# A decoder layer with product-key experts: one weight tile instead of two in the expert loop, seven gathered-row buffers instead of five, and another eviction order

## The chip, the cores and the metric

The kernel runs on one core of a Trainium2 chip. The metric is the device time of one execution in microseconds. Before the change it is 2859.01 us, the median of three runs (2856.11 to 2863.37).

## What is computed

One layer of a decoder on 1024 tokens of width 1024: RMS norm, four retention heads and four differential attention heads, an output projection with a residual, then a product-key expert layer (PEER) and a final norm. The change touches the expert layer alone:

```
def peer(xn, wq, subkeys, u, v):
    ...
        q = (xb @ wq).reshape(t, PEER_HEADS, 2, PEER_DQ // 2)
        s = jnp.einsum('thpd,hpkd->thpk', q, subkeys).astype(jnp.float32)
        s_top, i_top = lax.top_k(s, K)
        ...
        e = i1 * N_KEYS + i2
        g = jax.nn.softmax(c_top, axis=-1)
        ue = jnp.take(u, e, axis=0)
        ve = jnp.take(v, e, axis=0)
        act = jax.nn.gelu(jnp.einsum('thkd,td->thk', ue, xb).astype(jnp.float32), approximate=False)
        return jnp.einsum('thk,thkd->td', (g * act).astype(xb.dtype), ve)
```

Each token picks 8 x 16 = 128 of 16384 single-neuron experts; `u` and `v` have a row of 1024 floats for each.

## The kernel before

The eight tiles of 128 tokens go two ways. Three tiles are **sparse** (`ST`): POOL gathers for each of the 128 picks one row of `u` per token (line 869, a 128x1024 tile), and VectorE multiplies it with the token and sums (line 871); after a Gelu the rows of `v` follow (line 876), and VectorE adds each, times its weight, to the accumulator `sa` (line 878). All gathered rows live in the pool tag `ug` with five buffers; a gather waits until the update that reads the buffer's last row is done. Five tiles are **dense** (`DT`, 640 tokens): all 16384 experts are computed for them, in 128 blocks of 128 experts (a block is called an expert in the code), and a weight matrix G, zero where an expert was not picked, masks the result.

Two stages matter here. In the **G stage** (about 1010 to 1290 us) `dense_routes` and `build_g` make G: for eight tokens at a time VectorE makes one-hot tiles `oh` (lines 586 to 593, ScalarE helps on line 590), TensorE multiplies them (line 601) into a PSUM bank `psG` with four tokens of 128x128 each, and ScalarE evicts the bank into `st` (line 603), whose layout is expert block, then 32 tokens. `st` goes to DRAM as `g_d` (line 608). Woven into this are 39 expert blocks computed ahead (`spills`): load `uraw`, split it into a high and a low part (lines 711, 713), 48 products `psHs` (lines 725 to 727), Gelu by ScalarE (line 728), store to `hs_d`.

Then comes the **expert loop**, 32 groups of `EG` = 4 expert blocks. Each group loads its piece of G, `gt` (line 796, 128x2560 floats, 1280 KB). For each of its four blocks `ga` (computed, or read back as `gl` from `hs_d`, line 810, in three of four blocks of the first 13 groups) is multiplied with its part of `gt` (line 814, VectorE), split into `wh` and `wl` (lines 818, 820), and the block's rows of `v` are loaded and split into `vh` and `vl` (lines 822 to 826). Then 120 products per group (lines 802 to 804) add into four PSUM banks that are kept (`kp`) and six that VectorE adds to SBUF accumulators (`psV`, line 838). `gt` has two buffers, one in the pool `lp` and one in `dp`, used in turn.

The order on every engine is set by a scheduler that runs when the kernel is built: it lists the instructions by a plan of their times, with the sparse rows' updates held to follow certain VectorE instructions (`gate`). On the chip each engine then takes its list strictly in order. All plain loads and stores are issued by SP's queue, the gathers by POOL's.

Of the kernel before, what the change touches and what calls it, by code (L numbers as in the profile page):

```python
# [13 lines left out]
F32 = mybir.dt.float32  # L14
# [9 lines left out]
P = 128  # L24
T = 1024
D = 1024
# [5 lines left out]
HK = PH * K  # L32
# [11 lines left out]
GC = 32  # L44
NGC = TB // GC
GPAD = 64
EG = 4
KEEP = 4
RAW = 4
UG = 5  # L50
BIGS = 4
ROUTE = 6
MIX = 3
# [45 lines left out]
def layer_kernel(ctx, tc, x, wt, wn, wo, wq, sk, ut, u, v, gmix, gffn, gfin, gsub, dlam, consts, alb, out):  # L99
    nc = tc.nc  # L100
    V, A, PE, G, SY = nc.vector, nc.scalar, nc.tensor, nc.gpsimd, nc.sync
# [472 lines left out]
    def build_g(gp, pp, r, lo, tb):  # L574

        for s in range(P // GC):
            st = gp.tile([P, NK, GC], F32, tag="st", bufs=2, name="st")
            for q in range(GC // 8):
                blk = s * (GC // 8) + q
                oh = gp.tile([P, 4, 4, NK, 2], F16, tag="oh", bufs=3, name="oh")  # L580

                def tk(c0, c1):
                    n = 4 * (c1 - c0)
                    return r[:, blk, c0:c1].rearrange("p c (a b) -> p (c a) b", b=2)[:, :, None].to_broadcast([P, n, NK, 2])

                V.tensor_tensor(oh[:, 0:2].rearrange("p c a i b -> p (c a) i b"),
                                iop[:, None].to_broadcast([P, 8, NK, 2]), tk(0, 2), op=ALU.is_equal)
                V.tensor_tensor(oh[:, 2], oh[:, 1], tk(2, 3), op=ALU.mult)
                for tt in range(2 * ACTS):
                    A.activation(oh[:, 3, tt // 2, :, tt % 2], oh[:, 1, tt // 2, :, tt % 2], AF.Copy,  # L590
                                 scale=lo[:, blk, tt:tt + 1])
                if ACTS < 4:
                    V.tensor_tensor(oh[:, 3, ACTS:], oh[:, 1, ACTS:], tk(3, 4)[:, ACTS:], op=ALU.mult)
                for b in range(2):
                    with tc.high_priority(AHEAD):
                        tag = "BB" if q % 2 else "TR"
                        ps = pp.tile([P, 4, P], F32, tag=tag[b], bufs=1 + q % 2, name="psG")
                        for k in range(4):
                            tt = 4 * b + k
                            for c in (2, 3):  # L600
                                PE.matmul(ps[:, k], oh[:, 0, tt // 2, :, tt % 2], oh[:, c, tt // 2, :, tt % 2],
                                          start=(c == 2), stop=(c == 3))
                        A.activation(st[:, :, q * 8 + 4 * b:q * 8 + 4 * b + 4].rearrange("p i t -> p t i"), ps,
                                     AF.Copy, scale=1.0 / GS)
                yield
            c, n = tb * (P // GC) + s, NK // EG // 4
            for i in range(4):
                SY.dma_start(g_d[i * n:(i + 1) * n, :, c * EG * GC:(c + 1) * EG * GC].rearrange("g p x -> p g x"),
                             st[:, i * EG * n:(i + 1) * EG * n].rearrange("p (g e) t -> p g (e t)", e=EG))
# [42 lines left out]
    def pool(name, es=ctx, **kw):  # L652
        return es.enter_context(tc.tile_pool(name=name, bufs=1, reuse_waits="tile", **kw))
# [20 lines left out]
    def last_dve():  # L674
        ins = nc.cur_bb.bb.instructions
        return next(i for i in reversed(ins) if i.engine == V.engine).name

    def gated(g, per):

        due = 0.0  # L680
        for y in g:
            due += per[y == "turned"]
            while due >= 1.0:
                gates.append(last_dve())
                due -= 1.0
            yield y

    def run(g):
        for _ in g:
            pass  # L690

    def until(g, mark):
        for y in g:
            if y == mark:
                return
            yield y

    sp = pool("sp")
    lp = pool("lp")
# [39 lines left out]
    with ExitStack() as es:  # L739
        pf = pool("pf", es, space=bass.MemoryType.PSUM)  # L740
        ms, md = SimpleNamespace(), SimpleNamespace()
        with ExitStack() as e2:
            fs = pool("fs", e2)
            ms.tp = ms.vp = ms.fp = ms.hp = ms.np = md.tp = fs
            md.hp, md.np, md.vp = wp, wp, lp
            ug = ("ug", UG)
            ms.big = md.big = (sp, *ug)
# [10 lines left out]
        with ExitStack() as e2:  # L758
            fd = pool("fd", e2)
            md.tp = md.ap = md.fp = fd  # L760
            md.big = (fd, "big", BIGS)
            run(gated(weave(until(gd, "routing"), sparse_routes(sp, lates, s0, sn, ug, ug, ug), ROUTE, 1), PER[:2]))
# [7 lines left out]
    dp = pool("dp")  # L770
# [21 lines left out]
        SY.dma_start(acc[un], x2_d[DT[un[0]]][:, 512 * un[1]:512 * (un[1] + 1)])  # L792
    NG = NK // EG
    for g in range(NG):
        gt = (dp if g % 2 else lp).tile([P, NGC, EG, GC], F32, tag="rv", name="gt")
        SY.dma_start(gt.rearrange("p c e t -> p (c e t)"), g_d[g][:, :NGC * EG * GC])
        Wh, Wl, Vh, Vl = [], [], [], []

        def vmm(ps, un, e, start, stop):
            sl = slice(un[0] * P, (un[0] + 1) * P)  # L800
            so = slice(un[1] * 512, (un[1] + 1) * 512)
            PE.matmul(ps, Wh[e][:, sl], Vh[e][:, so], start=start, stop=False)  # L802
            PE.matmul(ps, Wh[e][:, sl], Vl[e][:, so], start=False, stop=False)  # L803
            PE.matmul(ps, Wl[e][:, sl], Vh[e][:, so], start=False, stop=stop)  # L804

        for e in range(EG):
            ei = g * EG + e
            if ei in early:
                ga = wp.tile([P, TB], F32, tag="ga", bufs=2, name="gl")
                SY.dma_start(ga, hs_d[early.index(ei)])  # L810
            else:
                ga = experts_in(ei, lambda hf: pd.tile([P, 512], F32, tag="H", bufs=2, name="psH"))
            gv = ga.rearrange("p (c t) -> p c t", t=GC)
            V.tensor_mul(gv, gv, gt[:, :, e])
            if ei == 0:
                gates.append(last_dve())
            wh = dp.tile([P, TB], F32R, tag="wh", bufs=EG + 1, name="wh")
            A.activation(wh, ga, AF.Copy)  # L818
            wl = wls[ei % (EG + 1)]
            V.tensor_sub(wl, ga, wh.bitcast(F32))  # L820
            vr = wp.tile([P, D], F32, tag="raw", bufs=RAW, name="vraw")
            SY.dma_start(vr, v[ei * P:(ei + 1) * P])
            vh = dp.tile([P, D], F32R, tag="vh", bufs=EG + 1, name="vh")
            A.activation(vh, vr, AF.Copy)  # L824
            vl = dp.tile([P, D], F32R, tag="vl", bufs=EG + 1, name="vl")
            V.tensor_sub(vl, vr, vh.bitcast(F32))  # L826
            Wh.append(wh), Wl.append(wl), Vh.append(vh), Vl.append(vl)
        for part in (units[:KEEP // 2], units[KEEP:], units[KEEP // 2:KEEP]):
            if part[0] in kept:
                for e in range(EG):  # L830
                    for un in part:
                        vmm(kept[un], un, e, g == 0 and e == 0, g == NG - 1 and e == EG - 1)
                continue
            for un in part:
                ps = pd.tile([P, 512], F32, tag="V", bufs=2, name="psV")
                for e in range(EG):
                    vmm(ps, un, e, e == 0, e == EG - 1)
                V.tensor_add(acc[un], ps, acc[un])  # L838
# [15 lines left out]
    def gate(ins):  # L854
# [3 lines left out]
                          reason="pace of the gathered experts")  # L858
        nth += 1

    for t in range(NS):
        xt = sp.tile([P, D], F32, tag="sx", name="sx")
        SY.dma_start(xt, xn_d[t])
        ac = sp.tile([P, D], F32, tag="sa", name="sa")
        SY.dma_start(ac, x2_d[ST[t]])
        hs = sp.tile([P, HK], F32, tag="shs", name="shs")
        for k in range(HK):
            ug = sp.tile([P, D], F32, tag="ug", bufs=UG, name="ug")
            G.indirect_dma_start(out=ug, out_offset=None, in_=u,  # L869
                                 in_offset=bass.IndirectOffsetOnAxis(ap=idxA[t][:, k:k + 1], axis=0))  # L870
            gate(V.scalar_tensor_tensor(ug, ug, 1.0, xt, op0=ALU.mult, op1=ALU.mult, accum_out=hs[:, k:k + 1]))  # L871
        A.activation(hs, hs, AF.Gelu)
        V.tensor_mul(hs, hs, gA[t])
        for k in range(HK):
            vg = sp.tile([P, D], F32, tag="ug", bufs=UG, name="vg")
            G.indirect_dma_start(out=vg, out_offset=None, in_=v,  # L876
                                 in_offset=bass.IndirectOffsetOnAxis(ap=idxA[t][:, k:k + 1], axis=0))
            gate(V.scalar_tensor_tensor(ac, vg, hs[:, k:k + 1], ac, op0=ALU.mult, op1=ALU.add))  # L878
        finish(sp, ac, ST[t], sp.tile([P, D], F32, tag="ug", bufs=UG, name="sfin"), gain(sp, "ug", UG))

# [37 lines left out]
```

## Time and profile before

| | |
|---|---|
| Median of three runs | 2859.01 us (2856.11 to 2863.37) |
| Profiled execution | 2852.44 us |
| Span of its instructions | 2850.7 us |
| TensorE busy | 2685.6 us (94%) |
| VectorE busy | 2305.2 us (81%) |
| ScalarE busy | 1063.0 us (37%) |
| POOL busy | 1058.6 us (37%) |
| DMA | 797.46 MB, 280 GB/s over the span |

Busy time is the union of an engine's instructions in the profiled execution. In the rows, PE is TensorE's products, PEld its weight loads, DVE VectorE, ACT ScalarE, POOL GpSimd, SPq the issuing queue of SyncE; L603 is line 603 of the kernel. An arrow names what ended a wait. "issue" is time for which the profile shows no cause.

### The profile page before, as it was taken

How to read it: one execution, taken by the hardware profiler on the slowest of the kernel's cores; microseconds unless marked ns; L12 is line 12 of the kernel's file. 1: busy time of each engine (PE TensorE's matmuls, PEld its weight loads, DVE VectorE, ACT ScalarE, POOL GpSimd, SP SyncE). 2: the span in 40 equal slices, each digit the busy share in tenths (PEclk: the TensorE clock that was granted, in tenths of full speed). 3: DMA queues.
4: the chain of work that ended last, by engine and by line, in shares of the span. 5: the costliest groups of instructions: out<-in, count | busy, mean ns of one | idle time of the engine just before them, and what ended most of it. 6: DMA issues, size and time to landing. Idle time of an engine off the chain costs nothing.

```text
span 2850.7 us, 43219 instructions
## 1 busy us (share of the span) xinstructions
PE 2685.6 (94%) x16043; PEld 2418.0 (85%) x16043; DVE 2305.2 (81%) x4495; ACT 1063.0 (37%) x1881; POOL 1058.6 (37%) x782
## 2 busy tenths in 40 slices
PE   7979988888889999998999999999999999999998
PEld 5858887776689999997788888998888899989887
DVE  3554789877578988985998988888888889888888
ACT  4653335554233369892222232322222222222212
POOL 0000003543310000002555545665565566665663
PEclk9989999999989999999999999999999999999999
DMA  7546556877854347788998999999999999989987
GB/s 249 194 172 214 198 201 245 303 273 248 310 184 134 113 150 240 231 259 317 336 352 336 337 346 334 341 332 337 322 328 335 331 338 349 349 311 338 328 316 258
DMA packets 302070, 797.46 MB, mean 280 GB/s; under 512 B 25113, under 2 KB 119321, under 8 KB 297762
## 3 DMA queue, kind: packets, MB, share of 16 engines
q0 software_dynamic: 111744, 404.28, 39.4%
q1 hardware_dynamic: 190114, 390.41, 38.8%
q8 instruction: 126, 2.06, 0.3%
q14 instruction: 86, 0.70, 0.1%
HBM read 698.97 MB, written 95.62 MB: 279 GB/s over the span
## 4 chain that ended last, share of the span: by engine, by line
PE 38%; DMA 13%; issue 13%; DVE 10%; POOL 9%; ACT 3%; SPq 0%; POOLq 0%; DVEq 0%; ACTq 0%
POOL vg L876 6%; DMA ug<-in_u,idx 5%; DMA vg<-in_v,idx 5%; PE psV L802 3%; PE psV L803 3%; PE psV L804 3%; DVE ug L871 3%; PE psH L725 3%; PE psH L726 3%; PE psH L727 3%; POOL ug L869 2%; PE psHs L725 2%; PE psHs L727 2%; PE psHs L726 2%; PE kp L804 2%
## 5 line engine op out<-in xcount | busy, mean ns | idle before, releaser
L876 POOL DMA_INDIRECT vg<-in_v,idx x384 | 544.4, 1418 | 883.1 <-DVE ug L871 519.4
L869 POOL DMA_INDIRECT ug<-in_u,idx x384 | 508.9, 1325 | 469.9 <-DVE ug L871 309.5
L878 DVE SCALAR_TENSOR_TENSOR sa<-vg,shs,sa 128x1024 f32<-128x1024 f32 x384 | 492.0, 1281 | 66.5 <-DMA vg<-in_v,idx 62.6
L871 DVE SCALAR_TENSOR_TENSOR ug<-ug,sx 128x1024 f32<-128x1024 f32 x384 | 460.7, 1221 | 97.4 <-DMA ug<-in_u,idx 94.9
L725 PE MATMUL psH<-nh,uh 128*128 128x320 f32 x1424 | 440.3, 309 | 8.2 <-ACT uh L711 4.3
L726 PE MATMUL psH<-nl,uh 128*128 128x320 f32 x1424 | 439.5, 309 | 0.0
L727 PE MATMUL psH<-nh,ul 128*128 128x320 f32 x1424 | 438.4, 309 | 0.4 <-DVE ul L713 0.4
L802 PE MATMUL psV<-vh,wh 128*128 128x512 f32 x768 | 301.4, 393 | 7.0 <-DVE accl L838 4.8
L803 PE MATMUL psV<-vl,wh 128*128 128x512 f32 x768 | 300.1, 391 | 0.0
L725 PEld LDWEIGHTS psH<-nh,uh 128*128 128x128 f32 x1424 | 267.3, 188 | 16.3 <-ACT ga L728 5.5
L726 PEld LDWEIGHTS psH<-nl,uh 128*128 128x128 f32 x1424 | 267.4, 188 | 5.2
L727 PEld LDWEIGHTS psH<-nh,ul 128*128 128x128 f32 x1424 | 267.0, 188 | 3.6 <-DVE ul L713 0.7
L728 ACT ACTIVATE ga<-psH 128x320 f32<-128x320 f32 x178 | 75.3, 426 | 396.0 <-PE psH L727 354.6
L711 ACT ACTIVATE uh<-uraw 128x1024 fp32r<-128x1024 f32 x128 | 135.8, 1061 | 210.8 <-PE psH L726 116.0
L725 PE MATMUL psHs<-nh,uh 128*128 128x320 f32 x624 | 196.9, 317 | 10.9 <-ACT ga L728 10.7
L803 PE MATMUL kp<-vl,wh 128*128 128x512 f32 x512 | 200.9, 393 | 1.3 <-DVE vl L826 1.3
L161 ACT ACTIVATE whi<-wraw 128x1024 fp32r<-128x1024 f32 x104 | 110.0, 1058 | 244.4 <-PE psT L170 129.2
L802 PE MATMUL kp<-vh,wh 128*128 128x512 f32 x512 | 192.3, 392 | 3.7 <-ACT wh L818 3.7
L726 PE MATMUL psHs<-nl,uh 128*128 128x320 f32 x624 | 194.6, 312 | 0.0
L727 PE MATMUL psHs<-nh,ul 128*128 128x320 f32 x624 | 193.2, 314 | 0.8 <-DVE ul L713 0.8
L824 ACT ACTIVATE vh<-vraw 128x1024 fp32r<-128x1024 f32 x128 | 131.2, 1052 | 162.5 <-PE psV L804 77.8
L713 DVE TENSOR_TENSOR ul<-uraw,uh 128x1024 fp32r<-128x1024 f32 x128 | 156.2, 1220 | 42.6 <-ACT uh L711 42.4
(251 smaller groups left out, 6148.6 us busy)
## 6 DMA issues: line engine op xcount, KB each, us to landing
uraw<-in_ut SPq DMA_DIRECT2D x128, 512.0 KB
vraw<-in_v SPq DMA_DIRECT2D x128, 512.0 KB
g_d<-st SPq DMA_DIRECT2D x80, 512.0 KB
gt<-g_d SPq DMA_DIRECT2D x32, 1280.0 KB
wl_d<-wlo SPq DMA_DIRECT2D x52, 512.0 KB
wlo<-wl_d SPq DMA_DIRECT2D x52, 512.0 KB
wraw<-in_wt SPq DMA_DIRECT2D x32, 512.0 KB
wraw<-in_wq SPq DMA_DIRECT2D x32, 512.0 KB
```

The costliest lines, as they stand in the source:

```text
L711: A.activation(uh, raw, AF.Copy)
L713: V.tensor_sub(ul, raw, uh.bitcast(F32))
L725: PE.matmul(ps, uh[:, dc], xh[:, dc, sl], start=(dc == 0), stop=False)
L726: PE.matmul(ps, uh[:, dc], xl[:, dc, sl], start=False, stop=False)
L727: PE.matmul(ps, ul[:, dc], xh[:, dc, sl], start=False, stop=(dc == DC - 1))
L802: PE.matmul(ps, Wh[e][:, sl], Vh[e][:, so], start=start, stop=False)
L803: PE.matmul(ps, Wh[e][:, sl], Vl[e][:, so], start=False, stop=False)
L804: PE.matmul(ps, Wl[e][:, sl], Vh[e][:, so], start=False, stop=stop)
L869: G.indirect_dma_start(out=ug, out_offset=None, in_=u, in_offset=bass.IndirectOffsetOnAxis(ap=idxA[t][:, k:k + 1], axis=0))
L871: gate(V.scalar_tensor_tensor(ug, ug, 1.0, xt, op0=ALU.mult, op1=ALU.mult, accum_out=hs[:, k:k + 1]))
L876: G.indirect_dma_start(out=vg, out_offset=None, in_=v, in_offset=bass.IndirectOffsetOnAxis(ap=idxA[t][:, k:k + 1], axis=0))
L878: gate(V.scalar_tensor_tensor(ac, vg, hs[:, k:k + 1], ac, op0=ALU.mult, op1=ALU.add))
```

## The change

The eviction on line 603 still moves the same bank to the same place, but walks expert by expert: it writes four neighbouring floats of `st` (four tokens of one expert) at a time and reads PSUM in steps of 128 floats. `gt` has one buffer, in `lp`. The room in `dp` goes to two further buffers for gathered rows, tag `ux`: for the second and third sparse tile, five of seven rows in turn use `ug` and two use `ux`; the first tile keeps five.

```
--- before.py
+++ after.py
@@ -48,6 +48,7 @@
 KEEP = 4
 RAW = 4
 UG = 5
+UX = 2
 BIGS = 4
 ROUTE = 6
 MIX = 3
@@ -600,7 +601,7 @@
                             for c in (2, 3):
                                 PE.matmul(ps[:, k], oh[:, 0, tt // 2, :, tt % 2], oh[:, c, tt // 2, :, tt % 2],
                                           start=(c == 2), stop=(c == 3))
-                        A.activation(st[:, :, q * 8 + 4 * b:q * 8 + 4 * b + 4].rearrange("p i t -> p t i"), ps,
+                        A.activation(st[:, :, q * 8 + 4 * b:q * 8 + 4 * b + 4], ps.rearrange("p t i -> p i t"),
                                      AF.Copy, scale=1.0 / GS)
                 yield
             c, n = tb * (P // GC) + s, NK // EG // 4
@@ -792,7 +793,7 @@
         SY.dma_start(acc[un], x2_d[DT[un[0]]][:, 512 * un[1]:512 * (un[1] + 1)])
     NG = NK // EG
     for g in range(NG):
-        gt = (dp if g % 2 else lp).tile([P, NGC, EG, GC], F32, tag="rv", name="gt")
+        gt = lp.tile([P, NGC, EG, GC], F32, tag="rv", name="gt")
         SY.dma_start(gt.rearrange("p c e t -> p (c e t)"), g_d[g][:, :NGC * EG * GC])
         Wh, Wl, Vh, Vl = [], [], [], []
 
@@ -858,6 +859,12 @@
                           reason="pace of the gathered experts")
         nth += 1
 
+    def row(t, i, name):
+
+        if t and i % (UG + UX) >= UG:
+            return dp.tile([P, D], F32, tag="ux", bufs=UX, name=name)
+        return sp.tile([P, D], F32, tag="ug", bufs=UG, name=name)
+
     for t in range(NS):
         xt = sp.tile([P, D], F32, tag="sx", name="sx")
         SY.dma_start(xt, xn_d[t])
@@ -865,14 +872,14 @@
         SY.dma_start(ac, x2_d[ST[t]])
         hs = sp.tile([P, HK], F32, tag="shs", name="shs")
         for k in range(HK):
-            ug = sp.tile([P, D], F32, tag="ug", bufs=UG, name="ug")
+            ug = row(t, k, "ug")
             G.indirect_dma_start(out=ug, out_offset=None, in_=u,
                                  in_offset=bass.IndirectOffsetOnAxis(ap=idxA[t][:, k:k + 1], axis=0))
             gate(V.scalar_tensor_tensor(ug, ug, 1.0, xt, op0=ALU.mult, op1=ALU.mult, accum_out=hs[:, k:k + 1]))
         A.activation(hs, hs, AF.Gelu)
         V.tensor_mul(hs, hs, gA[t])
         for k in range(HK):
-            vg = sp.tile([P, D], F32, tag="ug", bufs=UG, name="vg")
+            vg = row(t, HK + k, "vg")
             G.indirect_dma_start(out=vg, out_offset=None, in_=v,
                                  in_offset=bass.IndirectOffsetOnAxis(ap=idxA[t][:, k:k + 1], axis=0))
             gate(V.scalar_tensor_tensor(ac, vg, hs[:, k:k + 1], ac, op0=ALU.mult, op1=ALU.add))
```

All lines behind the new ones have other numbers: 603 is now 604, 796 is 797, 814 is 815, 869 and 876 are 876 and 883, 871 and 878 are 878 and 885.

The scheduler's order is the same up to the expert loop. In the loop it differs. VectorE in the fourth group, from the group's last multiply with `gt` (`ga<-ga,gt`) to the first two of the next (`gl<-gl,gt`); `sa<-vg` are updates with gathered rows, `wls` is one of the low parts. Before:

```order
L814 TENSOR_TENSOR ga<-ga,gt 128x640
L878 SCALAR_TENSOR_TENSOR sa<-vg,shs,sa 128x1024
L814 TENSOR_TENSOR gl<-gl,gt 128x640
L820 TENSOR_TENSOR wls<-ga,wh 128x640
L878 SCALAR_TENSOR_TENSOR sa<-vg,shs,sa 128x1024
L820 TENSOR_TENSOR wls<-gl,wh 128x640
L878 SCALAR_TENSOR_TENSOR sa<-vg,shs,sa 128x1024
L713 TENSOR_TENSOR ul<-uraw,uh 128x1024
L838 TENSOR_TENSOR accl<-psV,accl 128x512
L838 TENSOR_TENSOR accd<-psV,accd 128x512
L878 SCALAR_TENSOR_TENSOR sa<-vg,shs,sa 128x1024 x3
L814 TENSOR_TENSOR gl<-gl,gt 128x640
```

With the change:

```order
L815 TENSOR_TENSOR ga<-ga,gt 128x640
L885 SCALAR_TENSOR_TENSOR sa<-vg,shs,sa 128x1024
L821 TENSOR_TENSOR wls<-ga,wh 128x640
L885 SCALAR_TENSOR_TENSOR sa<-vg,shs,sa 128x1024 x2
L714 TENSOR_TENSOR ul<-uraw,uh 128x1024
L885 SCALAR_TENSOR_TENSOR sa<-vg,shs,sa 128x1024
L839 TENSOR_TENSOR accl<-psV,accl 128x512
L885 SCALAR_TENSOR_TENSOR sa<-vg,shs,sa 128x1024
L839 TENSOR_TENSOR accd<-psV,accd 128x512
L815 TENSOR_TENSOR gl<-gl,gt 128x640
L885 SCALAR_TENSOR_TENSOR sa<-vg,shs,sa 128x1024
L821 TENSOR_TENSOR wls<-gl,wh 128x640
```

The next group's first multiply stood behind one row update; now it stands behind five, a subtraction for `wls`, one for `ul`, and two accumulations.

SP's queue in the same part of the loop, from one load of `uraw` to the next, before:

```order
L709 DMA uraw<-in_ut 128x1024
L822 DMA vraw<-in_v 128x1024
L796 DMA gt<-g_d 128x2560
L810 DMA gl<-hs_d 128x640 x2
L822 DMA vraw<-in_v 128x1024 x2
L810 DMA gl<-hs_d 128x640
L822 DMA vraw<-in_v 128x1024
L709 DMA uraw<-in_ut 128x1024
```

With the change:

```order
L811 DMA gl<-hs_d 128x640
L823 DMA vraw<-in_v 128x1024
L797 DMA gt<-g_d 128x2560
L811 DMA gl<-hs_d 128x640
L823 DMA vraw<-in_v 128x1024
L811 DMA gl<-hs_d 128x640
L823 DMA vraw<-in_v 128x1024 x2
L710 DMA uraw<-in_ut 128x1024
```

One read-back `gl` and one `vraw` now go ahead of the load of `gt`, the other two `gl` behind it as before; before, the load was for the group after the next, now it is for the next.

POOL's gathers from the first tile's rows of `v` on (`idx_78` is the first sparse tile, `idx_79` the second), before:

```order
L876 DMA vg<-in_v,idx_78 128x1024 x128
L869 DMA ug<-in_u,idx_79 128x1024 x128
L876 DMA vg<-in_v,idx_79 128x1024 x128
L869 DMA ug<-in_u,idx_80 128x1024 x128
L876 DMA vg<-in_v,idx_80 128x1024 x128
```

With the change:

```order
L883 DMA vg<-in_v,idx_78 128x1024
L876 DMA ug<-in_u,idx_79 128x1024 x2
L883 DMA vg<-in_v,idx_78 128x1024 x127
L876 DMA ug<-in_u,idx_79 128x1024 x121
L883 DMA vg<-in_v,idx_79 128x1024
L876 DMA ug<-in_u,idx_79 128x1024
L883 DMA vg<-in_v,idx_79 128x1024
L876 DMA ug<-in_u,idx_79 128x1024 x4
L883 DMA vg<-in_v,idx_79 128x1024 x126
```

Two rows of the second tile are now gathered ahead of nearly all of the first tile's `v` rows, and where a tile goes over from `u` to `v`, two rows of `v` are gathered some places early.

## Rows read from the trace of the kernel before

**Rows 1.** Table of stretches (us: busy us of each engine, granted clock, DMA share, GB/s).

```profile
1040.00:1290.00 250.00, 241.15 (x2322) 230.77 (x2321) 218.36 (x303) 228.30 (x379) 0.00 (x0) 1.00 0.78 240
...
1310.00:1330.00 20.00, 14.89 (x69) 12.13 (x68) 12.32 (x17) 6.12 (x8) 5.71 (x4) 0.83 0.70 250
...
1400.00:1500.00 100.00, 100.00 (x487) 85.62 (x486) 93.14 (x96) 23.27 (x32) 61.13 (x39) 1.00 0.94 355
```

**Rows 2.** Groups of ScalarE by shape: count | busy us, mean ns | idle before, releasers.

```profile
L603 ACT ACTIVATE st<-psG 128x512 f32<-128x512 f32 x160 | 163.3, 1167 | 13.3 <-PE psG L601 13.2
...
L457 ACT ACTIVATE sc<-psc 128x512 f32<-128x512 f32 x16 | 9.6, 598 | 1.9 <-PE psc L455 1.9
...
L457 ACT ACTIVATE sc<-psc 128x128 f32<-128x128 f32 x16 | 4.4, 273 | 0.0
...
L562 ACT ACTIVATE rt<-psR 128x128 f16<-128x128 f32 x5 | 1.4, 271 | 0.0
```

**Rows 3.** The same view of VectorE, line 532.

```profile
L532 DVE COPY mz<-late 128x40 f32<-128x40 f32 x1 | 0.2, 181 | 0.0
...
L532 DVE COPY mz<-late 128x24 f32<-128x24 f32 x1 | 0.2, 161 | 0.0
```

**Rows 4.** Waits of the weight loads, 1040 to 1296: us in total, times, longest.

```profile
PEld psHs L725 <- ACT ga L728: 6.4, 10, 1.7
PEld L601 <- issue: 5.5, 9, 1.1
```

**Rows 5.** Timeline (start, us) of VectorE, 2703 to 2740: multiplies of line 814.

```profile
2704.89 0.82 DVE L814 TENSOR_TENSOR ga<-ga,gt 128x640 f32<-128x640 f32 x1
...
2737.02 0.81 DVE L814 TENSOR_TENSOR ga<-ga,gt 128x640 f32<-128x640 f32 x1
```

**Rows 6.** Timeline of VectorE and TensorE, 1372 to 1398 and at 1509.

```profile
1373.29 0.82 DVE L814 TENSOR_TENSOR ga<-ga,gt 128x640 f32<-128x640 f32 x1
...
1379.60 1.23 DVE L713 TENSOR_TENSOR ul<-uraw,uh 128x1024 fp32r<-128x1024 f32 x1 [0.72 <-ACT uh L711]
1380.74 0.82 DVE L820 TENSOR_TENSOR wl<-gl,wh 128x640 fp32r<-128x640 f32 x1
1381.48 1.28 DVE L878 SCALAR_TENSOR_TENSOR sa<-vg,shs,sa 128x1024 f32<-128x1024 f32 x1
1382.68 0.68 DVE L838 TENSOR_TENSOR accl<-psV,accl 128x512 f32<-128x512 f32 x1
1383.28 0.68 DVE L838 TENSOR_TENSOR accd<-psV,accd 128x512 f32<-128x512 f32 x1
...
1397.14 0.39 PE L802 MATMUL psV<-vh,wh 128*128 128x512 f32 x1
...
1509.36 0.82 DVE L814 TENSOR_TENSOR ga<-ga,gt 128x640 f32<-128x640 f32 x1
```

**Rows 7.** Timeline of the issuing queue SP at those two places.

```profile
1374.14 0.33 SPq L796 DMA_DIRECT2D gt<-g_d  x1
...
1510.20 0.33 SPq L796 DMA_DIRECT2D gt<-g_d  x1
```

**Rows 8.** DMA view of 1377.4 to 1386.2 and 1512.9 to 1519.2: packets by size.

```profile
DMA packets 820, 3.65 MB, mean 415 GB/s; under 512 B 80, under 2 KB 80, under 8 KB 691
...
DMA packets 486, 2.47 MB, mean 392 GB/s; under 512 B 48, under 2 KB 48, under 8 KB 358
```

**Rows 9.** Waits in the loop, 1290 to 2851: us in total, times, longest.

```profile
DVE sa L878 <- DMA vg<-in_v,idx: 62.6, 53, 4.8
DVE ug L871 <- DMA ug<-in_u,idx: 56.3, 48, 4.7
...
PE psV L802 <- DVE accl L838: 4.8, 7, 1.2
```

**Rows 10.** Timeline at the end: last row update, last product.

```profile
2832.61 1.28 DVE L878 SCALAR_TENSOR_TENSOR sa<-vg,shs,sa 128x1024 f32<-128x1024 f32 x1
...
2841.10 0.39 PE L804 MATMUL psV<-vh,wl 128*128 128x512 f32 x1
```

More of the change, by code (lines that the diff above doesn't have):

```diff
@@ L50 @@
 UG = 5
+UX = 2
 BIGS = 4
@@ L602, in build_g @@
                                           start=(c == 2), stop=(c == 3))
-                        A.activation(st[:, :, q * 8 + 4 * b:q * 8 + 4 * b + 4].rearrange("p i t -> p t i"), ps,
+                        A.activation(st[:, :, q * 8 + 4 * b:q * 8 + 4 * b + 4], ps.rearrange("p t i -> p i t"),
                                      AF.Copy, scale=1.0 / GS)
@@ L794, in layer_kernel @@
     for g in range(NG):
-        gt = (dp if g % 2 else lp).tile([P, NGC, EG, GC], F32, tag="rv", name="gt")
+        gt = lp.tile([P, NGC, EG, GC], F32, tag="rv", name="gt")
         SY.dma_start(gt.rearrange("p c e t -> p (c e t)"), g_d[g][:, :NGC * EG * GC])
@@ L859, in gate, with row @@
         nth += 1
+    def row(t, i, name):
+        if t and i % (UG + UX) >= UG:
+            return dp.tile([P, D], F32, tag="ux", bufs=UX, name=name)
+        return sp.tile([P, D], F32, tag="ug", bufs=UG, name=name)
     for t in range(NS):
@@ L867, in layer_kernel @@
         for k in range(HK):
-            ug = sp.tile([P, D], F32, tag="ug", bufs=UG, name="ug")
+            ug = row(t, k, "ug")
             G.indirect_dma_start(out=ug, out_offset=None, in_=u,
@@ L874, in layer_kernel @@
         for k in range(HK):
-            vg = sp.tile([P, D], F32, tag="ug", bufs=UG, name="vg")
+            vg = row(t, HK + k, "vg")
             G.indirect_dma_start(out=vg, out_offset=None, in_=v,
```

## The prediction

> **What bounds the kernel now.** I read the page first, where TensorE has by far the most busy time, then a table of stretches, which tells where that is a limit [rows 1], then the rows of the one stretch that the change touches first. From 1400 us on, in the dense expert loop, every stretch of 100 us reads within 4 us of the one shown: TensorE busy throughout, at full granted clock. What another engine saves there is worth nothing as long as TensorE never waits. In the stage before it (1040 to 1290 us: G is built from one-hot products while 39 experts are computed ahead) TensorE has 241 of 250 us, ScalarE 228 and VectorE 218: three engines close to full, coupled by small buffers. The start of the loop loses TensorE time and clock: the reader should see 14.89 busy of 20 us, and 0.83 of the clock, from 1310 to 1330 us.
>
> **Part 1, the eviction (line 603).** Nothing is added or moved; 160 ScalarE instructions change their form. Now each reads its PSUM bank in order and writes one float every 128 bytes of `st`. It takes 1167 ns, where the plain eviction of 128x512 on line 457 takes 598 [rows 2]: 569 ns per piece, 160 x 0.569 = 91 us of ScalarE. The new form writes runs of four floats (16 bytes) and reads one float every 512 bytes of PSUM. The writes have a near row: line 562 writes runs of eight f16 (16 bytes), from PSUM runs of eight floats, in 271 ns, where the plain 128x128 takes 273 [rows 2]. Such runs cost nothing. The reads have no row on this engine. The nearest is on VectorE from SBUF: line 532 copies every sixteenth float (64-byte hops), 24 of them in 161 ns and 40 in 181 ns, so 16 further elements cost 20 ns, 1.25 ns each [rows 3], no sign of a doubled price. So the ends are 598 ns (a read hop is free) and, at the top, the present 1167 ns plus a second penalty of the same 569 ns, some 1740 ns. I take 0.60 us, from the two rows nearest.
>
> [...]
>
> What 0.60 us is worth is not 91 us, since TensorE is the fuller engine. It is what TensorE now loses to ScalarE in the stage. Its weight loads sat idle 6.4 us in ten waits for line 728 (the experts' evictions, queued behind line 603 on ScalarE) and 5.5 us in nine waits at line 601 [rows 4]; together 11.9 us, 0.63 us a wait, about what one eviction gives back. I take -10 us, between 0 and -12.
>
> **Part 2, one buffer for `gt`.** No instruction is removed. The load of group g+1 (1280 KB) may now start only after the last multiply of group g, and the scheduler has moved the next group's first multiply behind more VectorE work. Two cases.
>
> In groups 13 to 31 the next first multiply comes long after: 2704.89 to 2737.02 us, 31.3 us after the end of the last one [rows 5]. A load of 9 to 12 us (below) is hidden there, and 0 is the cost. If that cover shrank below 12 us, VectorE would stand still.
>
> In the first twelve groups (experts read back from DRAM) the next group's first multiply now follows after one row update, and the order of the change puts five gathered-row updates, one 128x640 and one 128x1024 subtraction and two accumulations between them. By the spacings of the rows behind the multiply at 1373.29 us (1.20 us a row update, 0.74, 1.14, 0.60 us [rows 6]) that is 5 x 1.20 + 0.74 + 1.14 + 2 x 0.60 = 9.1 us. Against that stands the load. One was issued at 1374.14, right after the multiply, and another at 1510.20 [rows 7]. Packets of 8 KB and more are `gt`'s: 820 - 691 = 129 (one is an instruction fetch) between 1377.4 and 1386.2 us, and 486 - 358 = 128 between 1512.9 and 1519.2 [rows 8]; so it lands 12.1 and 9.0 us after its issue. VectorE arrives at 9.1 and stands still 0 to 3 us per group, eleven times. What waits behind it: gathered rows' updates, and TensorE, whose products of that group begin at 1397.14, 23 us after that multiply, and so some 10 us after the moved one [rows 6]. VectorE has 6.9 us free in the stretch of 100 us [rows 1], 2.3 us in a group of 34.0 (four groups lie between the last multiplies at 1373.29 and 1509.36 [rows 6]). On SP's queue the load holds back the expert loads behind it by nothing new: it is issued as soon as the multiply ends. I take +2 us for TensorE, between 0 and +22 (2 us in each of eleven groups).
>
> At the loop's start the second load of `gt` goes away, but the two new buffers let POOL issue two gathers of the second tile (512 KB each) ahead of the first tile's rows: 1280 KB less and 1024 KB more in a stretch in which the DMA engines are 0.70 busy [rows 1]. I take -1 us, between -8 (most of the 5.1 us of TensorE missing from 1310 to 1330, and some clock) and +4.
>
> **Part 3, seven row buffers.** The 768 gathers and their updates stay. In the loop VectorE waits 62.6 + 56.3 us for gathered rows [rows 9], and a deeper queue may take a part of that away for the second and third tile. TensorE sees little of it: its waits for VectorE's accumulation are 4.8 us in all [rows 9]. I take -2 us, between -5 and +3 (more gathers in flight also compete with the weight loads). At the end nothing is gained either: the last row update starts at 2832.61, and TensorE's last product at 2841.10 sets the end [rows 10].
>
> **Sum.** -10 + 2 - 1 - 2 = -11 us. The profiled execution took 2852.44 us (span 2850.7, 1.7 us around it), which gives 2841; it lies 6.6 us below the median of the runs, 2859.01, and the forecast is for that: 2859 - 11 = **2848 us**. A measurement of this kernel can tell 0.3%, 8.6 us, from no change.
>
> **The rivals.**
> A is the forecast, 2848 us, its own range 2838 to 2858. For it: TensorE's waits in the stage are on ScalarE. Against: the order was planned before, and other waits may take their place.
>
> B, **`gt` comes late**: slower. The place is the first multiply of groups 2 to 12 on VectorE, and the price its wait plus the lateness that it hands to TensorE. It decides where the load lands later than 9.1 + 2.3 = 11.4 us after the multiply; one of the two loads seen does. At 2 us in each of eleven groups it costs 22 where A has 2: 2848 + 20 = 2868 us. Against it: TensorE has some 10 us between the moved multiply and its use.
>
> C, **the eviction stays where it is**: reads pay what writes did, 1.17 us. Then part 1 is 0 and the time is 2858 us, no change. For it: no row shows a free read hop from PSUM.
>
> D, **the eviction costs more**: above a certain price ScalarE becomes the bound of the stage. It has 250 - 228.3 = 21.7 us free, 0.136 us for each of 160, so that point is 1.31 us. At 1.46 us (half a penalty more) it adds 160 x 0.29 = 46 us, less 21.7: 2859 + 24 = 2883 us; at 1.74 us 2859 + 70 = 2929.
>
> **How the numbers follow.** Chances: A 0.55, B 0.13, C 0.17, D 0.15. A is the likeliest, so 2848. The range takes in A, C and B and the lower bounds of the terms together: 2834 (A with the start at -8 and the buffers at -5, and a little more) to 2872; outside it are most of D and a little of A, below 2 in 10. Faster by over 8.6 us: two thirds of A, a fifth of C, a tenth of B, 0.42. Within: the rest of A, most of C and B, 0.40. Slower: nearly all of D, a fifth of B, a trace of C, 0.18.
>
> **What the profile will show.** Right: line 604 (603 now) at 0.6 us; ScalarE in the stage down from 228 to some 140 us; TensorE's waits at lines 601 and 725 there nearly gone; the first `gt` multiply of groups 2 to 12 about 10 us after the last one of the group before, with a wait of 0 to 3 us; TensorE still at 98 to 100 us of 100 in the loop. Wrong: line 604 at 1.1 us or more (C, D); or TensorE idle in 1400 to 1750 us behind line 815 and the weights made from it (B).

## The result, and the profile after

The change takes 2821.65 us (median; 2819.82 to 2828.0), the kernel before, run beside it, 2857.94 us (2856.11 to 2863.37). The ratio is 0.9884 with the interval [0.9862, 0.9907]: 36 us less, where 11 were forecast, and outside the range. Two further measurements, in which the kernel before stood at 2848.98 and 2847.27 us, gave 0.991 [0.9894, 0.9926] and 0.9922 [0.9907, 0.9938], 26 and 23 us less, which is about the lower end of the range. From the profile alone 31 us can be placed, as the text goes on to show; the profiled execution of before (2852.44 us) lies 3.5 and 5.2 us above its medians in those two measurements, which is part of the distance. The profiled execution took 2828.0 us, its span 2826.2; in it the part ahead of the G stage, where nothing is changed, happened to be 7.5 us longer than in the trace of before (in two further traces of the same kernel it is 0.9 and 1.9 us shorter), so spans are not subtracted here. Each stage is measured between two landmarks of its own trace instead.

The G stage first. Stretches of the changed kernel (columns as in [rows 1]: TensorE, weight loads, VectorE, ScalarE, POOL, then clock, DMA share, GB/s):

```profile
1040.00:1290.00 250.00, 249.72 (x2426) 242.75 (x2425) 223.66 (x317) 173.03 (x389) 1.87 (x2) 1.00 0.82 253
1310.00:1330.00 20.00, 15.45 (x73) 12.53 (x72) 16.57 (x22) 4.98 (x8) 12.47 (x8) 0.91 0.77 271
1400.00:1500.00 100.00, 100.00 (x493) 86.17 (x492) 91.85 (x95) 24.38 (x33) 60.14 (x39) 1.00 0.93 342
```

In 1040 to 1290 us TensorE had 241.15 us and 2322 products [rows 1]; now it has 249.72 and 2426. The line of the eviction, now 604, in ScalarE's groups by shape:

```profile
L604 ACT ACTIVATE st<-psG 128x512 f32<-128x512 f32 x160 | 85.3, 602 | 35.4 <-PE psG L602 35.2
```

It was 1167 ns [rows 2]. ScalarE now idles 35.2 us for TensorE's `psG` where it idled 13.2. Of TensorE's two waits in [rows 4], 6.4 and 5.5 us, this is left (weight loads, 1040 to 1296 us):

```profile
PEld psHs L726 <- ACT ga L729: 1.2, 2, 0.6
```

In the loop, the waits from 1290 us to the end, rows that answer to [rows 9] and some more:

```profile
DVE ug L878 <- DMA ug<-in_u,idx: 20.9, 15, 2.5
DVE sa L885 <- DMA vg<-in_v,idx: 8.3, 10, 1.7
ACT vh L825 <- DMA vraw<-in_v: 4.0, 4, 2.5
DVE gl L815 <- DMA gt<-g_d: 3.5, 3, 1.6
PE kp L803 <- ACT wh L819: 4.0, 2, 3.4
PE psV L803 <- DVE accl L839: 1.2, 1, 1.2
```

VectorE waited 62.6 + 56.3 us for gathered rows and now waits 8.3 + 20.9. The second thing to see is ScalarE's wait for the loads of `vraw`, 4.0 us. The same view of the kernel before has this, which I had not put among my rows:

```profile
ACT vh L824 <- DMA vraw<-in_v: 76.6, 29, 5.8
```

What TensorE got from it shows in two stretches of 500 us. Before:

```profile
1800.00:2300.00 500.00, 495.06 (x2774) 450.05 (x2773) 432.17 (x510) 127.86 (x184) 301.08 (x219) 1.00 0.91 332
2300.00:2800.00 500.00, 494.59 (x2768) 449.60 (x2768) 435.98 (x534) 123.57 (x178) 312.03 (x225) 1.00 0.91 332
```

After:

```profile
1800.00:2300.00 500.00, 500.00 (x2812) 456.35 (x2811) 437.86 (x520) 129.59 (x185) 311.81 (x224) 1.00 0.91 339
2300.00:2800.00 500.00, 500.00 (x2812) 456.39 (x2811) 439.86 (x523) 126.35 (x182) 313.89 (x221) 1.00 0.89 330
```

TensorE stood idle 4.94 + 5.41 = 10.3 of these 1000 us and now never does; it makes 5624 products in place of 5542, 1.5% or some 14.6 us of work more. The waits of TensorE in the same 1000 us of the kernel before are the whole of that idle time, 4.8 + 3.9 + 1.6 = 10.3 us; with the change this view is empty:

```profile
PE psV L802 <- DVE accl L838: 4.8, 7, 1.2
PE psH L725 <- ACT ga L728: 3.9, 4, 1.5
PE psV L802 <- DVE accS L838: 1.6, 1, 1.6
```

That is less than the 14.6 us by the products; the view of the products' waits does not show the rest. The waits of the weight loads in the same 1000 us have the same causes and come to 7.0 + 5.5 + 1.8 = 14.3 us, nearly all of it; with the change this view is empty too:

```profile
PEld psV L802 <- DVE accl L838: 7.0, 8, 1.5
PEld psH L725 <- ACT ga L728: 5.5, 6, 1.7
PEld psV L802 <- DVE accS L838: 1.8, 1, 1.8
```

**The landmarks.** "Stage" is from the first product `psG` to the loop's first `psH`, "early" from there to the last product of group 12 (groups are counted from 0; these are the 13 groups that read blocks back), "late" from there to the last product of the program. All in us but the eviction's mean; "rows" is VectorE's wait for gathered rows of `u` and `v` in the loop.

| kernel | row buffers, `gt` buffers | stage | early | late | eviction, ns | rows |
|---|---|---|---|---|---|---|
| before | 5, 2 | 302.9 | 473.4 | 1056.3 | 1167 | 118.9 |
| the change | 7, 1 | 287.5 | 474.0 | 1040.3 | 602 | 29.2 |
| e1_evict_only | 5, 2 | 288.0 | 471.2 | 1058.3 | 602 | 115.2 |
| e2_five_rows | 5, 1 | 286.1 | 467.1 | 1058.2 | 602 | 111.6 |
| e3_old_evict | 7, 1 | 300.1 | 475.3 | 1040.4 | 1174 | 32.6 |
| e4_six_rows | 6, 1 | 288.0 | 470.3 | 1041.1 | 602 | 49.3 |
| e7_four_rows | 4, 1 | 287.0 | 464.8 | 1134.0 | 602 | 200.6 |
| e8_ug6_ux1 | 7 (first tile 6), 1 | 287.1 | 473.3 | 1040.2 | 602 | 15.7 |
| e9_first_tile | 7 (first tile's `v` too), 1 | 289.4 | 484.2 | 1040.9 | 602 | 14.6 |

Of the change, 15.4 us come from the stage and 16.0 from the late groups; the early groups give +0.6.

### The profile page after: what moved, and what is told of

Read it like the earlier page. It is cut to its first block, busy times and chain, and to the rows that moved or that the text cites. A ratio compares the mean times of both kernels' runs of the same rounds, so it can differ in the third digit from the quotient of the medians.

```text
span 2826.2 us, 43137 instructions
## 1 busy us (share of the span) xinstructions
PE 2680.7 (95%) x16032; PEld 2419.8 (86%) x16043; DVE 2303.3 (81%) x4495; ACT 999.7 (35%) x1881; POOL 1065.7 (38%) x782
## 4 chain that ended last, share of the span: by engine, by line
PE 66%; DVE 8%; DMA 5%; issue 4%; POOL 1%; ACT 1%; POOLq 0%; DVEq 0%; ACTq 0%
PE psH L728 7%; PE psH L727 7%; PE psH L726 7%; PE psV L803 5%; PE psV L804 5%; PE psV L805 5%; PE kp L805 3%; PE kp L803 3%; PE kp L804 3%; PE psHs L726 3%; PE psHs L728 3%; PE psHs L727 3%; PE psG L602 3%; DVE ug L878 2%; DMA ug<-in_u,idx 2%
## 5 line engine op out<-in xcount | busy, mean ns | idle before, releaser
L876 POOL DMA_INDIRECT ug<-in_u,idx x384 | 524.9, 1367 | 913.9 <-ACT st L604 458.8
L883 POOL DMA_INDIRECT vg<-in_v,idx x384 | 535.4, 1394 | 394.4 <-DVE sa L885 293.1
L885 DVE SCALAR_TENSOR_TENSOR sa<-vg,shs,sa 128x1024 f32<-128x1024 f32 x384 | 492.1, 1281 | 12.8 <-DMA vg<-in_v,idx 8.3
L805 PE MATMUL psV<-vh,wl 128*128 128x512 f32 x456 | 173.8, 389 | 0.0
## 6 DMA issues: line engine op xcount, KB each, us to landing
gt<-g_d SPq DMA_DIRECT2D x32, 1280.0 KB, 10.1
```

Source lines behind the costliest of these rows:

```text
L876: G.indirect_dma_start(out=ug, out_offset=None, in_=u, in_offset=bass.IndirectOffsetOnAxis(ap=idxA[t][:, k:k + 1], axis=0))
L883: G.indirect_dma_start(out=vg, out_offset=None, in_=v, in_offset=bass.IndirectOffsetOnAxis(ap=idxA[t][:, k:k + 1], axis=0))
```

## The experiments

The theory was that the stage's gain is the eviction's and the late groups' gain is the row buffers', each by itself, and that `gt` costs nothing. The rivals: the eviction stands behind both gains (a freer ScalarE in the loop), or the single `gt` with the order that goes with it stands behind the loop's gain. No kernel below leaves out any of the computation.

**The eviction alone.** The kernel before, with the new line 603 only (two `gt` buffers, five rows, the old order):

```
-  A.activation(st[:, :, q * 8 + 4 * b:q * 8 + 4 * b + 4].rearrange("p i t -> p t i"), ps,
+  A.activation(st[:, :, q * 8 + 4 * b:q * 8 + 4 * b + 4], ps.rearrange("p t i -> p i t"),
```

> The kernel before with the new eviction alone (two gt buffers, five row buffers). In the two profiles the stage from the first one-hot product to the end of the experts computed ahead takes 301 us before and 287 us with the change, and the loop behind it 1530 and 1514 us. Theory 1 (the eviction gives about 14 us, the row buffers about 16): 14 us faster, ratio 0.995, the eviction at 0.60 us, the loop still about 1530 us with VectorE waiting some 120 us for gathered rows. Rival (the loop gained because the stage before it ends in another state, so the eviction is behind both gains): about 30 us faster, ratio 0.989, the loop at about 1514 us.

Measured: 2836.43 us, 0.9956 [0.994, 0.9972]. The stage has its whole gain, 302.9 to 288.0 us; the late groups have none.

**Five rows.** The change with its two further buffers unused, so that one `gt` and the new eviction stay:

```
-        if t and i % (UG + UX) >= UG:
+        if False:
```

> The changed kernel with five row buffers for every tile: one gt buffer and the new eviction stay. Theory 1 (the two further row buffers carry the loop's gain): 14 us faster than before, ratio 0.995, VectorE's waits for gathered rows back at some 120 us, the loop at about 1530 us. Rival (the loop gained from the one gt buffer, or from the new order that the scheduler wrote round it): about 30 us faster, ratio 0.989, the loop at about 1514 us. If the early loads of gt had been worth something, this kernel would be slower than 0.995.

Measured: 2834.57 us, 0.9954 [0.9941, 0.9967], as with the eviction alone. The late groups take 1058.2 us again. So neither the eviction nor the one `gt` moves them, and an order of its own does not either: VectorE's list in the late groups differs between the kernel before and this one. In this kernel's 1000 us (stretches, then waits in the loop) TensorE idles 8.4 us and makes 5572 products, and VectorE waits for rows as before:

```profile
1800.00:2300.00 500.00, 498.14 (x2797) 453.95 (x2796) 437.98 (x517) 130.75 (x186) 313.97 (x222) 1.00 0.92 337
2300.00:2800.00 500.00, 493.45 (x2775) 449.52 (x2774) 430.54 (x520) 122.61 (x177) 301.00 (x221) 1.00 0.90 327
```

```profile
DVE ug L878 <- DMA ug<-in_u,idx: 55.9, 42, 4.0
DVE sa L885 <- DMA vg<-in_v,idx: 55.7, 43, 3.3
PE psV L803 <- DVE accl L839: 7.0, 8, 1.6
```

**The old eviction** in the changed kernel, the diff of the first experiment turned round:

> The changed kernel with the old eviction: one gt buffer and seven row buffers stay. Theory 1: 16 to 19 us faster than before, ratio 0.994, the eviction at 1.17 us, the loop at about 1514 us. Rival (the eviction is behind both gains): no change, ratio 1.000, the loop at about 1530 us.

Measured: 2838.41 us, 0.9966 [0.9954, 0.9978]; stage 300.1, late groups 1040.4 us. The two gains are independent: each goes with its own edit. The time is 10 us less, where 16 to 19 were expected. By the medians the rows' part is 10 us here and 17 us between the kernel with five rows and the next one, with six; by the late groups of the traces it is 16 and 17. The difference in the medians is not explained.

**Six rows**, `UX = 1` in place of 2:

> The changed kernel with one further row buffer instead of two (six for the second and third tile). Theory 1, as a matter of how many rows are under way: between five and seven, VectorE's waits for gathered rows between 29 and 120 us, 20 to 28 us faster than before, ratio 0.990 to 0.993. Rival (the order the scheduler happens to write decides, not the number of buffers): the loop anywhere, for instance as short as with seven or as long as with five, and the waits not in line with the number of buffers.

Measured: 2817.39 us, 0.9895 [0.9876, 0.9914], 31 us less where 20 to 28 were expected. The sixth buffer brings the whole gain of the late groups, 1041.1 us, the seventh nothing that can be told apart, though it still shortens VectorE's waits (49.3 to 29.2 us). The rival of the order falls: in the late groups VectorE's list differs between six and seven rows, and the times are the same, while the waits for rows go with the number of buffers.

**Four rows.** To see whether the number of buffers sets the late time, one of five is taken away for the second and third tile (the final norm's scratch row is claimed when the second tile begins, and kept):

```
-        if t and i % (UG + UX) >= UG:
+        if False:
...
+    held = None
     for t in range(NS):
+        if t == 1:
+            held = gain(sp, "ug", UG)
...
-        finish(sp, ac, ST[t], sp.tile([P, D], F32, tag="ug", bufs=UG, name="sfin"), gain(sp, "ug", UG))
+        finish(sp, ac, ST[t], sp.tile([P, D], F32, tag="ug", bufs=UG, name="sfin"), held or gain(sp, "ug", UG))
```

> One gt buffer, new eviction, and only four buffers for the rows of the second and third tile (the fifth is held by the final norm's gain from the second tile on). Theory 1 as a count of rows under way: in the profile of the change a gathered row takes some 7.5 us from issue to landing, and issue on POOL (1.4 us), the update (1.3 us) and the hand-overs bring the round of one buffer to some 10.7 us; the loop wants a row each 2.2 us (441 rows in 980 us). Five buffers give one each 2.1 us, just enough, six 1.8 us, four only 2.7 us: VectorE must wait at nearly every row, and the late part of the loop grows from 1057 us to 1200 us or more, ratio 1.04 to 1.07. Rival (the written order decides): between no change and 20 us slower than with five, ratio 0.995 to 1.003.

Measured: 2913.06 us, 1.0203 [1.0167, 1.0239]; late groups 1134.0 us, 76 more than with five. The direction is as expected, the size is not: at least 1200 us were expected. The waits in the loop, and the DMA view of 1800 to 2780 us (count, median from issue to landing), tell more:

```profile
DVE sa L888 <- DMA vg<-in_v,idx: 102.8, 65, 5.4
DVE ug L881 <- DMA ug<-in_u,idx: 97.8, 76, 5.1
ACT vh L825 <- DMA vraw<-in_v: 141.0, 35, 8.3
PE psH L726 <- ACT ga L729: 28.0, 13, 4.0
PE psV L803 <- DVE accl L839: 15.8, 12, 2.7
```

```profile
vg<-in_v,idx POOLq DMA_INDIRECT x207, 6.3
ug<-in_u,idx POOLq DMA_INDIRECT x198, 6.4
```

A gather lands 6.3 to 6.4 us after its issue, where the same view has 7.0 and 7.4 with six buffers and 7.2 and 8.0 with seven. The 470 rows behind group 12 go at 1134.0 / 470 = 2.4 us each, so that one buffer is used again after 4 x 2.4 = 9.7 us; I had expected the round to stay at 10.7. By the same quotient a row takes 2.24 to 2.27 us with five, six and seven buffers: there, as TensorE hardly waits, the dense work sets the pace. TensorE loses 51 of 1000 us here:

```profile
1800.00:2300.00 500.00, 474.89 (x2573) 429.22 (x2573) 404.75 (x466) 117.49 (x169) 271.81 (x204) 0.97 0.87 306
2300.00:2800.00 500.00, 473.70 (x2616) 428.83 (x2616) 411.54 (x521) 118.67 (x172) 282.83 (x208) 0.99 0.88 314
```

**The change again**, on the chip of the four-row kernel and of the next two:

> The change itself once more, on the chip of the next three. Ratio 0.988 to 0.990, as measured first; the stage of the one-hot products near 287 us and the late part of the loop (groups 13 to 31) near 1040 us, where the kernel before takes 301 and 1056.

Measured: 2823.24 us, 0.991 [0.9894, 0.9926], a little above the expected 0.990; the stage takes 287.7 and the late groups 1039.9 us, as before.

**Seven buffers for the first tile's `v` rows too:**

```
-        if t and i % (UG + UX) >= UG:
+        if (t or i >= HK) and i % (UG + UX) >= UG:
```

> The change with seven buffers for the first tile's rows of v too (in the first twelve groups of the loop). Theory 1: VectorE waits less there, but TensorE lost only 0.2 to 2 us per 100 us in these groups, so no difference from the change, ratio 0.987 to 0.990. Rival (waits of VectorE for rows count wherever they stand): 5 to 10 us faster than the change, ratio 0.985.

Measured: 2839.16 us, 0.9966 [0.9953, 0.9978], so 16 us slower than the change, and a miss. The rows are hardly awaited any more, and yet the early groups take 484.2 us, against 475.7 in the change on the same chip: half of the difference (the part ahead of `psG` is 3.6 us longer, the stage 1.7). The scheduler has other places for the updates: in the trace, seven or eight of them stand between a group's last multiply with `gt` and the next group's first in groups 3 to 9, where the change has five, and the next multiply starts 13.4 to 15.8 us after the last, where it is 11.8 to 12.8 us in the change on the same chip. The weights come later (waits in the loop):

```profile
ACT wh L819 <- DVE gl L815: 200.2, 25, 20.4
DVE ug L878 <- DMA ug<-in_u,idx: 14.1, 10, 2.4
PE kp L803 <- ACT wh L819: 13.7, 5, 5.0
DVE sa L885 <- DMA vg<-in_v,idx: 0.5, 1, 0.5
```

With the change TensorE's wait for `wh` is 4.0 us and ScalarE's for `gl` is 118.3. So in the early groups the order seems to matter more than the buffers do; no kernel with these buffers and the old order was run. VectorE has 95.72 of the 100 us from 1400 on, where it had 91.85.

**A sixth buffer in `ug`, one in `ux`**, so that the first tile has six and the others seven; the room comes from a load buffer and one copy of `kn` in the sparse routing:

```
-UG = 5
-UX = 2
-BIGS = 4
+UG = 6
+UX = 1
+BIGS = 3
...
-                    kn = ap.tile([P, P], F32, tag="kn", bufs=2, name="kn")
+                    kn = ap.tile([P, P], F32, tag="kn", bufs=2 if dense else 1, name="kn")
```

> Seven row buffers for the second and third tile as in the change, but six of them from the start (UG 6, UX 1), so that the first tile's rows of u, gathered while the mixers run, have six; paid for with three instead of four buffers of the dense front and one instead of two of a small tile of the sparse front. If rows under way limit VectorE there too (before, it waited some 38 us for them ahead of the loop), up to 15 us faster than the change, ratio 0.984; if the dense front misses its fourth buffer, slower than the change, ratio 0.990 to 0.998.

Measured: 2814.95 us, 0.9875 [0.9854, 0.9896]: 8.3 us below the change on the same chip. To make sure of it, it was run again beside the change and beside a kernel that pays the price (`BIGS` and `kn`) with `UG` and `UX` as in the change:

> The kernel with six row buffers from the start and seven from the second tile on, once more, beside the change on the same chip. If its lead is one of the kernel and not of the chip: some 8 us (0.3%) under the change again.

> The change itself beside the two others, on the same chip: ratio 0.988 to 0.991, as in the two measurements so far.

> The change with only what that kernel pays: three instead of four buffers of the dense front, one instead of two of the small sparse tile, row buffers as in the change. If the lead comes from the sixth buffer for the first tile's rows of u: as slow as the change or up to 5 us slower. If the smaller front is itself faster (another order): as fast as the other kernel.

Measured: 2813.44 us, 0.9886 [0.9868, 0.9905]; the change 2824.32, 0.9922 [0.9907, 0.9938]; the price alone 2823.06, 0.9917 [0.9903, 0.9931]. The change came out a little above its expected range. The price costs nothing that can be told, and the sixth buffer is worth some 10 us. The largest part in the traces lies where the first tile's `u` rows are gathered, ahead of the G stage. There, 456 to 680 us, and VectorE's wait for rows from 456 to 850 us, with the sixth buffer:

```profile
456.00:680.00 224.00, 203.82 (x1306) 178.24 (x1315) 193.30 (x370) 119.11 (x313) 120.94 (x98) 0.96 0.82 287
```

```profile
DVE ug L878 <- DMA ug<-in_u,idx: 16.0, 9, 2.8
```

and in the change of the same set:

```profile
456.00:680.00 224.00, 197.79 (x1277) 172.27 (x1288) 189.76 (x363) 118.46 (x311) 115.20 (x98) 0.97 0.82 283
```

```profile
DVE ug L878 <- DMA ug<-in_u,idx: 33.7, 21, 4.7
```

TensorE has 6 us more of the 224. The first `psG` starts at 1002.4 us where it was 1006.9, and the early groups, with six buffers for the first tile's `v` rows, take 470.8 us where they took 474.1. This kernel has the lowest median of the study, and was faster than the change in both sets on the same chip.

Not tried: two `gt` buffers together with more than five row buffers; in the change the further row buffers take the room of the second `gt`.

## Why the prediction was wrong, step by step

**What bounds the kernel** was right as far as TensorE goes, but read too coarsely. "Every stretch of 100 us reads within 4 us of the one shown" was taken as "never waits". Those few microseconds, 10.3 in 1000, were what there was to gain.

**Part 1** had the right mechanism and the right price, 0.60 us forecast and 602 ns measured. Its worth was mis-sized: -10 us, between 0 and -12, where the stage gave -15.4 and the eviction alone -14.9. The term was the sum of two waits of the weight loads. The idle time of TensorE in the stretch was 8.85 us of 250, but the gain in products there is 104 of 2426, some 10.7 us of 250, and the stage is 288 long. For the whole stage that is 10.7 x 288 / 250 = 12.3 us, so that some 3 us of the gain have no row here. The gain is above the time of the waits, which I had used as its upper bound. ScalarE fell to 173 us and not to 140. The forecast multiplied 160 by a duration; but the evictions overlap one another (160 of 1167 ns are 186.7 us in 163.3 us of busy time), and by the busy time of their row they gave back 163.3 - 85.3 = 78 us, not 91, of which this stretch saw 73; and ten further instructions of ScalarE came into the stretch (389 in place of 379), and less overlaps: the durations there add up to 293 us in 228.3 us of busy time before, and to 212 in 173.0 with the change.

Rival C, by which the reads pay what the writes did, falls: ScalarE read one float every 512 bytes of PSUM at 602 ns, where the plain eviction takes 598 [rows 2]. Such reads cost nothing that can be told here. With C, rival D (a still higher price) falls too.

**Part 2** was right in that a late `gt` costs nothing, though VectorE comes to it later than forecast: VectorE waits 3.5 us in all for the late `gt`, in three waits, and TensorE's waits for the weights made from it are 4.0 us where they were 3.7. The timeline of VectorE and the issue on SP after the second group, the place that the forecast worked from:

```profile
1364.36 0.82 DVE L815 TENSOR_TENSOR ga<-ga,gt 128x640 f32<-128x640 f32 x1
...
1373.77 2.60 DVE L885 SCALAR_TENSOR_TENSOR sa<-vg,shs,sa 128x1024 f32<-128x1024 f32 x2
1376.29 0.82 DVE L815 TENSOR_TENSOR gl<-gl,gt 128x640 f32<-128x640 f32 x1
```

```profile
1365.20 0.33 SPq L797 DMA_DIRECT2D gt<-g_d  x1
```

```profile
gt<-g_d SPq DMA_DIRECT2D x32, 1280.0 KB, 10.1
```

The multiply starts 11.9 us after the last one, and the load, issued at 1365.20, lands 10.1 us later by the median: just ahead of it. The forecast had 9.1 us for the work between; the last multiply itself and VectorE's idle 1.93 us ahead of `ul` (it waited for ScalarE's `uh`) make up the rest. After the third to tenth group it is 11.8 to 13.5 us. Rival B needed a landing later than 11.4 us after the multiply. That happened: loads issued at 1465.58, 1499.91 and 1672.13 us took 11.0, 11.6 and 14.7 us, from an issue 0.8 to 0.9 us after the start of the multiply. It cost next to nothing because VectorE came later too. The cost was 0 where +2 was taken: the early groups show +0.6 us, and with five rows one `gt` takes 4.1 us less there than two (467.1 and 471.2). **The loop's start** gave nothing that can be told (-1 forecast): from the first `psH` to the first product with `vh` it is 11.0 us before, and 10.6, 11.1 and 10.1 in three traces of the change.

**Part 3 is the step that failed**: "TensorE sees little of it: its waits for VectorE's accumulation are 4.8 us in all [rows 9]." It took -2 us, between -5 and +3, and the late groups gave -16. Its upper end was put down to gathers that compete with the weight loads, and no run shows that as a loss: with four, six and seven buffers a load of `vraw` lands 6.6, 6.7 and 7.0 us after its issue by the median of 1800 to 2780 us, and ScalarE's wait for it in the loop falls from 141.0 to 15.8 and 4.0 us. One row was taken for all that TensorE loses to late gathers. Its waits for `ga` and for `accS`, 3.9 + 1.6 us, belong to it as well, and the weight loads' waits of 14.3 us in 1000 were the better measure. With six or seven buffers all of them go; with five they stay, whichever of the other edits is made (13.9 us with the eviction alone, 11.3 with five rows and one `gt`).

How a late row reaches TensorE can be read in the trace of before, in two ways. The short way, at 2099 us: VectorE stands 4.78 us at a gathered row, its accumulation comes right behind, and TensorE waits for that.

```profile
2097.14 1.29 DVE L878 SCALAR_TENSOR_TENSOR sa<-vg,shs,sa 128x1024 f32<-128x1024 f32 x1 [4.78 <-DMA vg<-in_v,idx]
2098.35 0.68 DVE L838 TENSOR_TENSOR accl<-psV,accl 128x512 f32<-128x512 f32 x1
...
2099.09 0.51 PE L802 MATMUL psV<-vh,wh 128*128 128x512 f32 x1 [1.25 <-DVE accl L838]
```

All eight waits of TensorE for `accl` and `accS` in these 1000 us have VectorE waiting for a gathered row shortly ahead of the accumulation. The long way, at 2066 us: VectorE waits for a row and works without a pause up to `vl`; that frees the load buffer, and SP issues the next load of `vraw` 0.03 us after `vl` ends. ScalarE stands 5.48 us for this load, its Gelu `ga` (line 728) stands behind in its list, and TensorE waits for `ga`.

```profile
2051.69 2.60 DVE L878 SCALAR_TENSOR_TENSOR sa<-vg,shs,sa 128x1024 f32<-128x1024 f32 x2 [1.43 <-DMA vg<-in_v,idx]
...
2056.01 1.22 DVE L826 TENSOR_TENSOR vl<-vraw,vh 128x1024 fp32r<-128x1024 f32 x1
...
2057.26 0.33 SPq L822 DMA_DIRECT2D vraw<-in_v  x1
...
2064.36 1.06 ACT L824 ACTIVATE vh<-vraw 128x1024 fp32r<-128x1024 f32 x1 [5.48 <-DMA vraw<-in_v]
2065.32 0.42 ACT L728 ACTIVATE ga<-psH 128x320 f32<-128x320 f32 x1
...
2065.79 0.41 PE L725 MATMUL psH<-nh,uh 128*128 128x320 f32 x1 [1.16 <-ACT ga L728]
```

All four waits for `ga` there have ScalarE waiting for `vraw` just ahead of the Gelu. That the gathered rows are behind the whole of ScalarE's wait for `vraw` is not shown link by link; it goes with them: 141.0 us with four buffers, 76.6 before, 15.8 with six, 4.0 with seven.

**The sum** by the landmarks: -15.4, +0.6 and -16.0, some -31 us, where -11 were forecast; the medians of the three sets gave -36, -26 and -23.

## What to carry to other kernels

For an engine that is said to be busy all the time, count what it completes in a fixed stretch and add up all its waits; one releaser's row is a part of the loss, and 1% of idle time over a long loop can be the whole gain. For gathered rows, compare the time one buffer needs for a round with the number of buffers times the interval at which rows are wanted: here four were far too few, five cost 1.5% of the late groups, six were enough. By the averages five should have been just enough (11.3 us for five rows, a round of some 10.7 as I estimated it ahead of the four-row run); equal averages leave nothing for a row that lands late. And where more buffers let a scheduler move work ahead, look at what it now puts behind it: with fewer waits for data the kernel can still be slower.

## What the runs showed of the hardware

On ScalarE the side that writes was what cost: single floats 128 bytes apart into SBUF 1167 ns for 128x512, runs of 16 bytes 602 ns, although each element is then read 512 bytes from the last one in PSUM. And a gather of 512 KB landed sooner with four buffers (6.3 and 6.4 us by the median) than with six (7.0 and 7.4) or seven (7.2 and 8.0); the DMA engines were also less busy there (0.87 and 0.88 of two stretches of 500 us, where the change has 0.91 and 0.89), and the two are not told apart. With it, taking one buffer of five away cost 76 us of the loop rather than the 140 and more expected.
